# Seven block products for the up projections, and a normalization in place, in a two-layer trunk on one core

## The chip, the cores and the metric

The kernel runs on one core of one Trainium2 chip. The metric is the device time of one execution in microseconds. The profile pages and views come from one profiled execution; the names PE, PEld, DVE, ACT, POOL and SP stand for TensorE's matmuls, its weight loads, VectorE, ScalarE, GpSimd and SyncE. L12 is line 12 of the kernel.

## The reference

The input is x of shape (1, 512, 1024) in float32. Two layers follow; each has a mixer and a gated feed-forward network (FFN), both with an RMS norm ahead and a residual added behind. What the change touches is the FFN, the same in both layers, with 2816 hidden channels:

```python
def rms_norm(x, g):
    y = x * lax.rsqrt(jnp.mean(x * x, axis=-1, keepdims=True) + EPS)
    return y * g

def gated_conv_ffn(x, w_gate, w_up, conv_w, conv_b, w_down):
    g = jnp.einsum('bsd,df->bsf', x, w_gate)
    g = causal_dwconv3(g, conv_w) + conv_b          # three taps along the sequence
    up = jnp.einsum('bsd,df->bsf', x, w_up)
    return jnp.einsum('bsf,fd->bsd', jax.nn.silu(g) * up, w_down)

# in each layer, after its mixer:
hn = rms_norm(h, norm_ffn[layer])
h = h + gated_conv_ffn(hn, w_ffn_gate[layer], w_ffn_up[layer], conv_ffn[layer],
                       b_conv_ffn[layer], w_ffn_down[layer])
```

A final RMS norm gives the output.

## The kernel before, in words

The residual lies in SBUF as eight tiles `h[k]` of 128 channels by 512 positions. Every operand of a matmul is kept as two float32r tiles, a high half (a rounded copy, made by ScalarE) and a low half (the rest, a subtraction on VectorE). `mm3` (L125 to L128) makes one product of three matmuls: high by high, high by low, low by high. So each 128 x 128 x 512 product costs three matmuls of 512 columns.

`Norm.add` runs as each residual tile is finished: it writes `hg[k]`, the two halves of the tile times the norm's gain, and adds the tile's square to `ssq` (ScalarE squares, POOL adds). The factor rstd of each position is not in `hg`; it is multiplied in after the matmuls. `Norm.rstd` (L178) makes it as a tile of 128 x 512: two matmuls by a tile of ones, and then `inv_sqrt` on full tiles.

The FFN goes through 11 groups of two hidden tiles (f = 0, 2, ..., 20). `gate_up` fetches four weight tiles of 512 KB (the gate and up columns, in two halves of the channels) through a ring of four `raw` buffers on SP's queue, and `parts` (L118) splits each into a pair `whi`, `wlo`, from rings of five. Then it makes 96 matmuls into four PSUM banks: two gate tiles, two up tiles. Group 0 interleaves the four banks (tail 4), the others finish bank by bank. `done` takes each bank out: a gate bank is multiplied by rstd (L465), goes through the convolution (`conv3`, L231 to L233, VectorE), the silu (L469, ScalarE) and a product with rstd (L470, POOL); an up bank is multiplied with that (L474) and `split` gives the activation's two halves. After 12 groups' tiles, and again after the last 10 (`HALVES`), the down projection runs over the tiles so far: `project` in layer 0 (names d), `group8` over eight banks in layer 1 (names dn). In layer 1 the residual is also transposed back (`turn_residual`, 32 transposes named hT) between the groups f = 2 to 8.

The order of the instructions on each engine is fixed when the program is built: a scheduler takes them by the order written, and puts a later one first where an earlier one would have to wait. Buffers of one tag are handed out as they come free.

Of the kernel before, what the change touches and what calls it, by code (L numbers as in the profile page):

```python
# [15 lines left out]
P = 128  # L16
# [14 lines left out]
def tile_trunk(ctx: ExitStack, tc: tile.TileContext, x, norm_mix, norm_ffn, final_norm,  # L31
# [52 lines left out]

    def params(layer, rows_, queue=nc.sync):
        rows = sum(n for _, _, n in rows_)
        pk = cp.tile([P, P], F32, tag=f"pk{layer}", name=f"pk{layer}")
# [12 lines left out]

        return col
# [13 lines left out]
    def weights(src, a, b, name):  # L115
        return parts(*fetch(src, a, b, name))

    def parts(raw, a, b, name):  # L118
        hi = wp.tile([P, a, b], F32R, tag="whi", bufs=5, name=f"whi_{name}")
        lo = wp.tile([P, a, b], F32R, tag="wlo", bufs=5, name=f"wlo_{name}")  # L120
        nc.scalar.activation(hi, raw, AF.Copy)  # L121
        nc.vector.tensor_tensor(lo, raw, hi.bitcast(F32), ALU.subtract)  # L122
        return hi, lo
# [3 lines left out]
        nc.tensor.matmul(ps, lhs[0], rhs[1], start=False, stop=False)  # L127
        nc.tensor.matmul(ps, lhs[1], rhs[0], start=False, stop=stop)  # L128

    def group(name, outs, ks, lhs, rhs, tail, on_done, before=None):  # L130

        banks = {}
        head = len(ks) - tail
# [3 lines left out]
        for i, j in order:  # L137
            if i > at and before is not None:
                before(ks[i])
            at = max(at, i)  # L140
            if j not in banks:
                banks[j] = mm_bank(f"{name}_{j}")
            mm3(banks[j], lhs(ks[i], j), rhs(ks[i], j), i == 0, i == len(ks) - 1)
            if i == len(ks) - 1:
                on_done(j, banks[j])


    h = [cp.tile([P, S], F32, name=f"h{k}") for k in range(NK)]
# [6 lines left out]
    class Norm:  # L155


        def __init__(self, name, gain):
            self.name, self.gain, self.n = name, gain, 0
            self.ssq = tp.tile([P, S], F32, tag="ssq", bufs=1, name=f"ssq_{name}")  # L160

        def add(self, k):
# [6 lines left out]
        def square(self, k, order=lambda ins: ins):  # L169
            if self.n == 0:  # L170
                order(nc.scalar.activation(self.ssq, h[k], AF.Square))
            else:
                sq = tp.tile([P, S], F32, tag="sq", name=f"sq_{self.name}{k}")
                order(nc.scalar.activation(sq, h[k], AF.Square))
# [2 lines left out]

        def rstd(self):  # L178
            ps = aux_bank(f"ss_{self.name}")
            hi = tp.tile([P, S], F32R, tag=f"ms{S}", bufs=1, name=f"ssh_{self.name}")  # L180
            lo = tp.tile([P, S], F32R, tag=f"sd{S}", bufs=1, name=f"ssl_{self.name}")
# [6 lines left out]
            return r  # L188

        def rstd_cols(self):  # L190
# [3 lines left out]
                                 ones, start=True, stop=True)  # L194
            return inv_sqrt_cols(ps[:, :NT], NT, f"{self.name}c")

    def newton(ms, n, name, r):


        sd = tp.tile([P, max(n, LINE)], F32, tag=f"sd{max(n, LINE)}", bufs=1, name=f"sd_{name}")[:, :n]  # L200
# [4 lines left out]

    def inv_sqrt(r, ss, n, name):

        ms = tp.tile([P, max(n, LINE)], F32, tag=f"ms{max(n, LINE)}", bufs=1, name=f"ms_{name}")[:, :n]
# [98 lines left out]
    def mixer0():  # L307
        nonlocal prm0
        w = w_in_even[0]
        with tc.tile_pool(name="m0", bufs=1) as mp:  # L310
# [116 lines left out]

            in_group("ab", w, 0, True, b_done, 4)

            nxt = Norm("f0", lambda k: prm0("ffn", k))  # L430
# [6 lines left out]
    def gate_up(layer, prm, rstd, ap, acts, f, tail):  # L437

        cs = slice(f * P, (f + 2) * P)
        ch = {}  # L440
        for half in range(2):
            for key, w in (("g", w_ffn_gate), ("u", w_ffn_up)) if tail < NK else ():
                ch[key, half] = weights(w[layer][half * 512 : (half + 1) * 512, cs]
                                        .rearrange("(k p) c -> p k c", p=P), 4, 256,
                                        f"{key}{layer}_{f}_{half}")
        if tail == NK:
            for key, w in (("g", w_ffn_gate), ("u", w_ffn_up)):
                for half in range(2):
                    ch[key, half] = weights(w[layer][half * 512 : (half + 1) * 512, cs]
                                            .rearrange("(k p) c -> p k c", p=P), 4, 256,  # L450
                                            f"{key}{layer}_{f}_{half}")

        def lhs(k, j):
            hi, lo = ch["gu"[j // 2], k // 4]
            c = slice((j % 2) * P, (j % 2 + 1) * P)
            return hi[:, k % 4, c], lo[:, k % 4, c]

        gates = {}

        def done(j, ps):  # L460
            ft = f + j % 2
            r = rstd()
            if j < 2:
                t = padded_tile()
                nc.vector.tensor_tensor(t[:, 2:], ps, r, ALU.mult)  # L465
                c = ap.tile([P, S], F32, tag="c", bufs=2, name=f"c{layer}_{ft}")
                conv3(c, t, *(prm("cf", i * NF + ft) for i in range(3)))
                s = ap.tile([P, S], F32, tag="s", bufs=3, name=f"s{layer}_{ft}")
                nc.scalar.activation(s, c, AF.Silu, bias=prm("bf", ft))  # L469
                nc.gpsimd.tensor_tensor(s, s, r, ALU.mult)  # L470
                gates[j] = s
            else:
                s = gates[j - 2]
                nc.vector.tensor_tensor(s, ps, s, ALU.mult)  # L474
                acts[ft] = split(ap, s, f"a{layer}_{ft}", tag="a", bufs=12)

        group(f"gu{layer}_{f}", range(4), list(range(NK)), lhs, lambda k, j: hg_k(k), tail, done)

    def lazy_rstd(norm):
        got = []  # L480

        def get():
            if not got:
                got.append(norm.rstd())
            return got[0]

        return get

    def ffn0(norm):
        nonlocal prm1  # L490
        with tc.tile_pool(name="f0", bufs=1) as ap:
            rstd = lazy_rstd(norm)
            nxt = None
            for a, b in HALVES:
                acts = {}
                for f in range(a, b, 2):
                    gate_up(0, prm0, rstd, ap, acts, f, 4 if f == 0 else NK)
# [3 lines left out]
                project(f"d0_{a}", w_ffn_down[0], acts, list(range(a, b)), nxt)  # L501
            return nxt


    def mixer1(norm):
        w = w_in_odd[0]
        with tc.tile_pool(name="m1", bufs=1) as mp:
# [113 lines left out]
                    for j in ((4,), (5,), (6, 7))[k - 1]:  # L621
                        turned(j)

            nxt = Norm("f1", lambda k: prm1("ffn", k))
            project("oo", w_out_odd[0], mix, list(range(NK)), nxt, before=second_half)
            return nxt


    def ffn1(norm):
        with tc.tile_pool(name="f1", bufs=1) as ap:  # L630
            fin = ap.tile([P, D], F32, name="fin")
            nc.scalar.dma_start(fin, final_norm.rearrange("(o d) -> o d", o=1).to_broadcast([P, D]))
            rstd = lazy_rstd(norm)
# [3 lines left out]
            def turn_residual(t):  # L637
                for half in range(2):
                    ps = mm_bank(f"hT{t}_{half}")
                    for i in range(4):  # L640
                        nc.tensor.transpose(ps[:, i * P : (i + 1) * P],
                                            h[half * 4 + i][:, t * P : (t + 1) * P], ident)
                    nc.scalar.copy(y[t][:, half * 512 : (half + 1) * 512], ps)

            for a, b in HALVES:
                acts = {}
                for f in range(a, b, 2):
                    gate_up(1, prm1, rstd, ap, acts, f, 4 if f == 0 else NK)
                    if 2 <= f <= 8:
                        turn_residual((f - 2) // 2)  # L650
                last = b == NF
                if last:
                    root = small[:, 2:3]
                    nc.scalar.activation(root, eps, AF.Sqrt)
                ch = {}
# [88 lines left out]
```

## Time and profile before

| | |
|---|---|
| median of three runs | 1020.78 us (1020.74 to 1020.91) |
| the profiled execution | 1023.1 us, its span 1021.4 us |
| granted TensorE clock | 0.998 of full |
| hidden groups in layer 0 | from 147.98 and from 344.27 us |
| down projections in layer 0 | from 278.99 and from 453.11 us |
| hidden groups in layer 1 | from 651.04 and from 850.97 us |
| down projections in layer 1 | from 785.69 and from 959.77 us |
| DMA | 101.24 MB, mean 99 GB/s |

A group's row on the page gives the busy time, the mean length of one instruction and the idle time of the engine before it. Matmuls overlap: a record of 390 ns says how long one was in the array, not how often one can start.

### The profile page before, as it was taken

The page shows a single profiled execution, that of the slowest core. Times are in us where ns is not written, and L with a number is a line of the kernel's source. Part 1 is how long each engine was busy: PE and PEld are TensorE (multiplying, and loading weights), DVE is VectorE, ACT ScalarE, POOL GpSimd, SP SyncE. Part 2 cuts the span into 40 slices and gives each one's busy share as a digit, 9 for nine tenths or more (in the row PEclk, how much of TensorE's full clock was granted, in tenths as well). Part 3 has the DMA queues.
Part 4 walks back from the last instruction along what each step waited for, and adds up shares of the span by engine and source line. Part 5 has one row for each costly group of instructions (what it writes and reads, how often), then busy time and mean ns, then how long its engine had stood idle before and what let it go on. Part 6 is the DMA issues. An engine that isn't in the chain of part 4 may idle for free.

```text
span 1021.4 us, 11177 instructions
## 1 busy us (share of the span) xinstructions
PE 1009.4 (99%) x4485; PEld 832.4 (81%) x4485; DVE 559.0 (55%) x706; ACT 345.3 (34%) x449; POOL 126.7 (12%) x113
## 2 busy tenths in 40 slices
PE   9999999999999999999999999999999999999997
PEld 6788888888888888888878888888888888888885
DVE  5997567755623455654423645486554226565526
ACT  5423443323312223333345444433332212332313
POOL 3141121111100011111110001211111001111100
PEclk9999999999999999999999999999999999999999
DMA  7432233332333332332333123324233224233302
GB/s 232 154 103 83 83 103 98 92 115 89 95 111 84 96 109 83 103 104 78 106 126 103 62 91 96 103 83 124 83 103 103 84 81 124 83 104 103 100 3 83
DMA packets 74719, 101.24 MB, mean 99 GB/s; under 512 B 3268, under 2 KB 52652, under 8 KB 74668
## 3 DMA queue, kind: packets, MB, share of 16 engines
q1 hardware_dynamic: 73324, 98.96, 31.2%
q10 hardware_dynamic: 1344, 1.58, 0.5%
q8 instruction: 35, 0.57, 0.2%
q14 instruction: 16, 0.13, 0.0%
HBM read 98.42 MB, written 2.10 MB: 98 GB/s over the span
## 4 chain that ended last, share of the span: by engine, by line
PE 97%; DVE 1%; DMA 1%; issue 0%; POOL 0%; ACT 0%; DVEq 0%; POOLq 0%; ACTq 0%
PE gu L127 16%; PE gu L128 16%; PE gu L126 16%; PE dn L127 4%; PE d L126 4%; PE d L128 4%; PE dn L128 4%; PE d L127 4%; PE dn L126 4%; PE oo L128 1%; PE u L127 1%; PE u L126 1%; PE oo L127 1%; PE u L128 1%; PE oe L127 1%; PE oe L126 1%
## 5 line engine op out<-in xcount | busy, mean ns | idle before, releaser
L126 PE MATMUL gu<-hgh,whi_g 128*128 128x512 f32 x352 | 137.3, 390 | 0.0
L128 PE MATMUL gu<-hgh,wlo_g 128*128 128x512 f32 x352 | 137.0, 389 | 0.0
L128 PE MATMUL gu<-hgh,wlo_u 128*128 128x512 f32 x352 | 137.0, 389 | 0.0
L127 PE MATMUL gu<-hgl,whi_g 128*128 128x512 f32 x352 | 136.9, 389 | 0.0
L126 PE MATMUL gu<-hgh,whi_u 128*128 128x512 f32 x352 | 136.9, 389 | 0.0
L127 PE MATMUL gu<-hgl,whi_u 128*128 128x512 f32 x352 | 136.9, 389 | 0.0
L470 POOL TENSOR_TENSOR s<-s,rstd_f 128x512 f32<-128x512 f32 x44 | 66.5, 1512 | 529.8 <-ACT s L469 529.8
L121 ACT ACTIVATE whi_g<-raw_g 128x1024 fp32r<-128x1024 f32 x44 | 46.6, 1059 | 169.9 <-PE gu L127 107.8
L122 DVE TENSOR_TENSOR wlo_u<-raw_u,whi_u 128x1024 fp32r<-128x1024 f32 x52 | 63.8, 1229 | 59.5 <-ACT whi_u L121 59.1
L122 DVE TENSOR_TENSOR wlo_g<-raw_g,whi_g 128x1024 fp32r<-128x1024 f32 x44 | 54.4, 1236 | 47.3 <-ACT whi_g L121 46.9
L126 PEld LDWEIGHTS gu<-hgh,whi_u 128*128 128x128 f32 x352 | 66.1, 188 | 13.8
L127 PEld LDWEIGHTS gu<-hgl,whi_u 128*128 128x128 f32 x352 | 66.1, 188 | 13.7
L128 PEld LDWEIGHTS gu<-hgh,wlo_g 128*128 128x128 f32 x352 | 66.1, 188 | 13.7
L126 PEld LDWEIGHTS gu<-hgh,whi_g 128*128 128x128 f32 x352 | 66.1, 188 | 13.6
L128 PEld LDWEIGHTS gu<-hgh,wlo_u 128*128 128x128 f32 x352 | 66.1, 188 | 13.6
L127 PEld LDWEIGHTS gu<-hgl,whi_g 128*128 128x128 f32 x352 | 66.1, 188 | 13.6
L121 ACT ACTIVATE whi_u<-raw_u 128x1024 fp32r<-128x1024 f32 x52 | 55.0, 1059 | 58.6 <-PE gu L127 20.7
L126 PE MATMUL d<-a_hi,whi_d 128*128 128x512 f32 x176 | 68.6, 390 | 0.0
L128 PE MATMUL d<-a_hi,wlo_d 128*128 128x512 f32 x176 | 68.5, 389 | 0.0
L127 PE MATMUL d<-a_lo,whi_d 128*128 128x512 f32 x176 | 68.5, 389 | 0.0
L126 PE MATMUL dn<-whi_dn,a_hi 128*128 128x512 f32 x176 | 68.5, 389 | 0.0
L127 PE MATMUL dn<-wlo_dn,a_hi 128*128 128x512 f32 x176 | 68.5, 389 | 0.0
(236 smaller groups left out, 1772.5 us busy)
## 6 DMA issues: line engine op xcount, KB each, us to landing
raw_g<-in_w_ffn_gate_dram SPq DMA_DIRECT2D x44, 512.0 KB
raw_u<-in_w_ffn_up_dram SPq DMA_DIRECT2D x44, 512.0 KB, 3.9
raw_d<-in_w_ffn_down_dram SPq DMA_DIRECT2D x22, 512.0 KB, 3.5
raw_dn<-in_w_ffn_down_dram SPq DMA_DIRECT2D x22, 512.0 KB, 3.3
raw_oe<-in_w_out_even_dram SPq DMA_DIRECT2D x8, 512.0 KB, 3.3
raw_v<-in_w_in_odd_dram SPq DMA_DIRECT2D x8, 512.0 KB, 3.6
raw_u<-in_w_in_odd_dram SPq DMA_DIRECT2D x8, 512.0 KB, 3.5
raw_oo<-in_w_out_odd_dram SPq DMA_DIRECT2D x8, 512.0 KB, 3.3
```

Of the source, the lines that this page charges most:

```text
L121: nc.scalar.activation(hi, raw, AF.Copy)
L122: nc.vector.tensor_tensor(lo, raw, hi.bitcast(F32), ALU.subtract)
L126: nc.tensor.matmul(ps, lhs[0], rhs[0], start=start, stop=False)
L127: nc.tensor.matmul(ps, lhs[0], rhs[1], start=False, stop=False)
L128: nc.tensor.matmul(ps, lhs[1], rhs[0], start=False, stop=stop)
L470: nc.gpsimd.tensor_tensor(s, s, r, ALU.mult)
```

## The change

- From the third group on (f = 4 and up, nine groups in each layer) the up half is computed by a block scheme of seven products (`seven`). The up weights and the normalized tiles are cut in 2 x 2 blocks: the weights in two halves of the channels by two hidden tiles, the tiles in the same halves of the channels by two halves of the positions (256). Seven products of sums of blocks give the four blocks of the result. The sums of weight blocks (`s23`, `s14`) are made by VectorE in each group, the sums of the tiles (`t23`, `t41`) once per layer. The products 1, 6, 7 and 4 are added up in one PSUM bank, which is copied out in between (`keep`), 5 and 3 in another.
- The tiles must be normalized for that. `normalize(kp)` makes `hg[kp]` and `hg[kp + 4]` anew with rstd in them, in place, and the sums. It is written three times before and once after the evacuation of group 0 (`rest()`). Group 0 still works with rstd behind the matmuls, group 2 with normalized tiles and its gates ahead of its ups.
- `rstd` comes from 8 matmuls of one column (`rstd_tokens`), the root on 128 x 4, and four transposes that spread it (`rstd_spread`), at positions 2 and 4 of group 0. The last square is kept apart instead of added by POOL.
- Low halves of the tile sums and of one up weight half come from a DMA on POOL's queue that adds into its destination. The convolution's first step moves from VectorE to ScalarE. POOL's product with rstd remains in group 0 alone.
- The down projection runs in four parts (`PARTS`) instead of two. In layer 1 all residual transposes move into group 0. Some buffers share places: `t23` of layer 1 takes those of `h`; `final_norm` is loaded late.

```diff
-    HALVES = ((0, 12), (12, 22))
+    PARTS = ((0, 6), (6, 12), (12, 18), (18, 22))
+    HALF = S // 2
+    NP = NK // 2
+    PAIRS = [k for i in range(NP) for k in (i, i + NP)]
...
+    def summed(raw, a, b, name):
+        hi = wp.tile([P, a, b], F32R, tag="whi", bufs=5, name=f"whi_{name}")
+        lo = wp.tile([P, a, b], F32R, tag="wlo", bufs=5, name=f"wlo_{name}")
+        nc.scalar.activation(lo, raw, AF.Copy, scale=-1.0)
+        nc.gpsimd.dma_start(lo, raw, accum_op=ALU.add)
+        nc.scalar.activation(hi, raw, AF.Copy)
+        return hi, lo
...
+        def rstd_tokens(self):
+            ps = aux_bank(f"sst_{self.name}")
+            for t in range(NT):
+                ts_ = slice(t * P, (t + 1) * P)
+                nc.tensor.matmul(ps[:, t : t + 1], self.ssq[:, ts_], ones, start=True, stop=False)
+                nc.tensor.matmul(ps[:, t : t + 1], self.last[:, ts_], ones, start=False, stop=True)
+            self.cols = inv_sqrt_cols(ps[:, :NT], NT, f"{self.name}t")
...
+        def normalize(self, kp):
+            n, r = f"{self.layer}_{kp}", self.r
+            x = self.ap.tile([P, 2, S], F32, tag="sum", bufs=3, name=f"x{n}")
+            for i, k in enumerate((kp, kp + NP)):
+                nc.vector.scalar_tensor_tensor(x[:, i, :], h[k], self.prm("ffn", k), r,
+                                               op0=ALU.mult, op1=ALU.mult)
...
+            halves(hg[kp], x[:, 0, :])
+            halves(hg[kp + NP], x[:, 1, :])
...
+            nc.vector.tensor_tensor(t[:, 1, :], b22, b12, ALU.subtract)
+            nc.vector.tensor_tensor(t[:, 0, :], t[:, 1, :], b11, ALU.add)
+            nc.vector.tensor_tensor(t[:, 3, :], b12, b11, ALU.subtract)
+            nc.vector.tensor_tensor(t[:, 2, :], b21, t[:, 0, :], ALU.subtract)
...
+            for (hi, lo), src in ((self.t23[kp], t[:, :2, :]), (self.t41[kp], t[:, 2:, :])):
+                nc.scalar.activation(lo, src, AF.Copy, scale=-1.0)
+                nc.gpsimd.dma_start(lo, src, accum_op=ALU.add)
+                nc.scalar.activation(hi, src, AF.Copy)
...
+        def seven(self, f):
...
+            gate = [parts(*raws["g", 0])]
...
+            nc.vector.tensor_tensor(s14[:, 0], r0[:, :, P:], r1[:, :, P:], ALU.add)
+            nc.vector.tensor_tensor(s23[:, 0], s14[:, 0], r0[:, :, :P], ALU.subtract)
+            nc.vector.tensor_tensor(s23[:, 1], r0[:, :, :P], r0[:, :, P:], ALU.subtract)
...
+            gate.append(parts(*raws["g", 1]))
+            nc.vector.tensor_tensor(s14[:, 1], r1[:, :, :P], s23[:, 0], ALU.subtract)
...
+            hi, lo = summed(*raws["u", 1])
...
+            def multiply(product):
...
+                ps = banks[at][:, :HALF]
+                hi, lo = stat[product]
+                for kp in range(NP):
+                    b_hi, b_lo = self.moving(product, kp)
+                    a_hi, a_lo = hi[:, kp, :], lo[:, kp, :]
+                    for l, r, end in ((a_hi, b_hi, False), (a_hi, b_lo, False),
+                                      (a_lo, b_hi, kp == NP - 1)):
+                        nc.tensor.matmul(ps, l, r, start=at not in opened, stop=end,
+                                         skip_group_check=True)
+                        opened.add(at)
+                return ps
...
+            keep(0, multiply(1))
+            gates(0)                     # pairs 0, 4, 1, 5 of the channels
+            keep(1, multiply(6))
+            gates(1)                     # pairs 2, 6, 3, 7
...
+            keep(2, multiply(7))
...
+            ps = multiply(5)
+            p2 = multiply(2)
+            add(2, ps)
+            add(0, p2)
+            ps = multiply(4)
...
+            self.act(f + 1, s[1])
+            add(1, multiply(3))
...
+            self.act(f, s[0])
+
+        def hidden(self, f, before=lambda i: None):
+            if f == 0:
+                def first(i):
+                    before(i)
+                    if i == 2:
+                        self.norm.rstd_tokens()
+                    elif i == 4:
+                        self.r = self.norm.rstd_spread()
+
+                rest = self.direct(0, False, (range(4),), first)
+                for kp in range(NP - 1):
+                    self.normalize(kp)
+                rest()
+                self.normalize(NP - 1)
+            elif f == 2:
+                self.direct(2, True, ((0, 1), (2, 3)))()
+            else:
+                self.seven(f)
```

`direct(f, normed, sets)` is the former scheme with the channel tiles in the order of `PAIRS` (0, 4, 1, 5, 2, 6, 3, 7); `sets` says which banks are made together.

More of the change, by code (lines that the diff above doesn't have):

```diff
@@ L86, in params @@
         rows = sum(n for _, _, n in rows_)
-        pk = cp.tile([P, P], F32, tag=f"pk{layer}", name=f"pk{layer}")
+        pk = cp.tile([P, P], F32, tag="pk", bufs=1, name=f"pk{layer}")
         at, views = 0, {}
@@ L128, in mm3, with group @@
         nc.tensor.matmul(ps, lhs[1], rhs[0], start=False, stop=stop)
-    def group(name, outs, ks, lhs, rhs, tail, on_done, before=None):
+    def group(name, outs, ks, lhs, rhs, tail, on_done, before=None, at_end=None):
         banks = {}
@@ L143, in group @@
             mm3(banks[j], lhs(ks[i], j), rhs(ks[i], j), i == 0, i == len(ks) - 1)
-            if i == len(ks) - 1:
+            if i == len(ks) - 1 and at_end is None:
                 on_done(j, banks[j])
-    h = [cp.tile([P, S], F32, name=f"h{k}") for k in range(NK)]
+        if at_end is not None:
+            at_end()
+            for j in outs:
+                on_done(j, banks[j])
+    h = [cp.tile([P, S], F32, tag=f"h{k}", name=f"h{k}") for k in range(NK)]
     hg = [(cp.tile([P, S], F32R, name=f"hgh{k}"), cp.tile([P, S], F32R, name=f"hgl{k}"))
@@ L171, in square @@
                 order(nc.scalar.activation(self.ssq, h[k], AF.Square))
+            elif self.n == NK - 1 and self.apart:
+                self.last = tp.tile([P, S], F32, tag="last", bufs=1, name=f"last_{self.name}")
+                order(nc.scalar.activation(self.last, h[k], AF.Square))
             else:
@@ L188, in rstd, with rstd_spread @@
             return r
+        def rstd_tokens(self):
[5 more added lines that the diff above has]
+            self.cols = inv_sqrt_cols(ps[:, :NT], NT, f"{self.name}t")
+        def rstd_spread(self):
+            ps = aux_bank(f"ssr_{self.name}")
+            for t in range(NT):
+                nc.tensor.transpose(ps[:, t * P : (t + 1) * P],
+                                    self.cols[:, t : t + 1].to_broadcast([P, P]), ident)
+            r = tp.tile([P, S], F32, tag="rstd", name=f"rstd_{self.name}")
+            nc.scalar.copy(r, ps)
+            return r
         def rstd_cols(self):
@@ L206, in inv_sqrt @@
     def inv_sqrt(r, ss, n, name):
-        ms = tp.tile([P, max(n, LINE)], F32, tag=f"ms{max(n, LINE)}", bufs=1, name=f"ms_{name}")[:, :n]
+        ms = work("ms", n, name)
         nc.vector.tensor_scalar(ms, ss, 1.0 / D, EPS, op0=ALU.mult, op1=ALU.add)
@@ L428, in mixer0 @@
             in_group("ab", w, 0, True, b_done, 4)
-            nxt = Norm("f0", lambda k: prm0("ffn", k))
+            nxt = Norm("f0", lambda k: prm0("ffn", k), apart=True)
             project("oe", w_out_even[0], mix, [4, 5, 6, 7, 0, 1, 2, 3], nxt)
             return nxt
-    HALVES = ((0, 12), (12, 22))
-    def gate_up(layer, prm, rstd, ap, acts, f, tail):
-        cs = slice(f * P, (f + 2) * P)
[L440 to L463, printed above, removed]
-                t = padded_tile()
[L465 to L471, printed above, removed]
-            else:
[L473 to L487, printed above, removed]
+    PARTS = ((0, 6), (6, 12), (12, 18), (18, 22))
+    HALF = S // 2
+    NP = NK // 2
+    PAIRS = [k for i in range(NP) for k in (i, i + NP)]
+    def ffn_weights(layer, f, order):
+        cs = slice(f * P, (f + 2) * P)
+        return {(key, half): fetch(
+            (w_ffn_gate if key == "g" else w_ffn_up)[layer][half * 512 : (half + 1) * 512, cs]
+            .rearrange("(k p) c -> p k c", p=P), 4, 256, f"{key}{layer}_{f}_{half}")
+            for key, half in order}
@@ L491, in ffn0, with sums @@
         with tc.tile_pool(name="f0", bufs=1) as ap:
-            rstd = lazy_rstd(norm)
+            def sums(kp):
+                return [ap.tile([P, 2, HALF], F32R, name=f"t23{i}_{kp}") for i in "hl"]
+            ffn = Ffn(0, prm0, norm, ap, sums)
             nxt = None
-            for a, b in HALVES:
-                acts = {}
+            for a, b in PARTS:
                 for f in range(a, b, 2):
-                    gate_up(0, prm0, rstd, ap, acts, f, 4 if f == 0 else NK)
+                    ffn.hidden(f)
                 if b == NF:
@@ L500, in ffn0 @@
                     nxt = Norm("m1", lambda k: prm1("mix", k))
-                project(f"d0_{a}", w_ffn_down[0], acts, list(range(a, b)), nxt)
+                project(f"d0_{a}", w_ffn_down[0], ffn.acts, list(range(a, b)), nxt)
             return nxt
@@ L630, in ffn1, with sums, turn_residual, before @@
         with tc.tile_pool(name="f1", bufs=1) as ap:
-            fin = ap.tile([P, D], F32, name="fin")
-            nc.scalar.dma_start(fin, final_norm.rearrange("(o d) -> o d", o=1).to_broadcast([P, D]))
-            rstd = lazy_rstd(norm)
+            def sums(kp):
+                return [cp.tile([P, 2, HALF], F32R, tag=f"h{k}", name=f"t23_{k}")
+                        for k in (kp, kp + NP)]
+            ffn = Ffn(1, prm1, norm, ap, sums)
+            acts = ffn.acts
             y = [ap.tile([P, D], F32, name=f"y{t}") for t in range(NT)]
             ssf = ap.tile([P, NT, PAD], F32, name="ssf")[:, :, :2]
[L637 to L646, printed above, removed]
+            def turn_residual(t, half):
+                ps = mm_bank(f"hT{t}_{half}")
+                for i in range(4):
+                    nc.tensor.transpose(ps[:, i * P : (i + 1) * P],
+                                        h[half * 4 + i][:, t * P : (t + 1) * P], ident)
+                nc.scalar.copy(y[t][:, half * 512 : (half + 1) * 512], ps)
+            def before(k):
+                if k < 4:
+                    turn_residual(k, 0)
+                elif k < 8:
+                    turn_residual(k - 4, 1)
+            for a, b in PARTS:
                 for f in range(a, b, 2):
-                    gate_up(1, prm1, rstd, ap, acts, f, 4 if f == 0 else NK)
-                    if 2 <= f <= 8:
-                        turn_residual((f - 2) // 2)
+                    ffn.hidden(f, before=before)
                 last = b == NF
                 if last:
+                    fin = wp.tile([P, D], F32, tag="raw", bufs=4, name="fin")
+                    nc.scalar.dma_start(
+                        fin, final_norm.rearrange("(o d) -> o d", o=1).to_broadcast([P, D]))
                     root = small[:, 2:3]
```

141 lines of the change are left out of this document (135 added, 6 removed).

## The prediction

> **What bounds the kernel now.** I read the page first, then what TensorE waits for, then its timeline, then VectorE's groups, then the stretches by time. The page:
>
> ```profile
> PE 1009.4 (99%) x4485; PEld 832.4 (81%) x4485; DVE 559.0 (55%) x706; ACT 345.3 (34%) x449; POOL 126.7 (12%) x113
> ...
> PE 97%; DVE 1%; DMA 1%; issue 0%; POOL 0%; ACT 0%; DVEq 0%; POOLq 0%; ACTq 0%
> ```
>
> The second line is the chain that ended last: 97% TensorE. All its waits on other engines are in the start-up (clock, z) and at the head of mixer 1 (wst):
>
> ```profile
> PE wst L520 <- POOL ws L513: 1.5, 1, 1.5
> PE clock L56 <- DVE idle L53: 1.3, 1, 1.3
> PE z L126 <- ACT hgh L342: 1.1, 2, 0.8
> PE z L127 <- DVE hgl L344: 0.8, 1, 0.8
> ```
>
> Inside both FFNs TensorE never stops. So time is won only by TensorE occupying less time, and any wait that appears is lost in full. TensorE's price per matmul is the distance between starts, not the 390 ns of a record:
>
> ```profile
> 300.07 0.39 PE L126 MATMUL d<-a_hi,whi_d 128*128 128x512 f32 x1
> 300.30 0.39 PE L127 MATMUL d<-a_lo,whi_d 128*128 128x512 f32 x1
> ...
> 300.98 0.39 PE L127 MATMUL d<-a_lo,whi_d 128*128 128x512 f32 x1
> ```
>
> Four starts in 0.91 us: 0.2267 us for 512 columns. Short matmuls, from the chain in order of time:
>
> ```profile
> 528.18 0.79 PE ssc_m L193 x8
> ...
> 763.21 0.88 PE hT L641 x8
> ```
>
> With 128 columns (hT) one costs 0.109 us, with 1 column (ssc) 0.099 to 0.112: a floor that doesn't depend on the columns, so it belongs to the weight load that every matmul carries. And VectorE in the first two hidden groups of layer 0:
>
> ```profile
> 148.00:170.00 22.00, 22.00 (x99) 18.23 (x98) 14.79 (x13) 6.91 (x9) 2.55 (x2) 1.00 0.35 100
> 170.00:192.00 22.00, 22.00 (x99) 18.23 (x98) 19.57 (x27) 9.90 (x13) 6.89 (x4) 1.00 0.31 92
> ```
>
> The columns after the length are PE, PEld, DVE, ACT and POOL busy. VectorE already works 34.4 of these 44 us, and the change adds work just there.
>
> **Block products.** In 9 of 11 groups of each layer (18 in all) the up half, 48 matmuls of 512 columns (48 x 0.2267 = 10.88 us), becomes seven products of 4 x 3 = 84 matmuls of 256 columns. The gate half stays. No matmul of 256 columns is in the trace. Bounds: not under the floor, 0.109; not over the straight line between 0.109 at 128 and 0.2267 at 512 columns, which gives 0.148, if the price is a flat floor and then a slope. If all of 0.2267 shrinks with the columns it is 0.113. I take 0.120, from the start-up, where the same 512 columns go at one in 0.43 us:
>
> ```profile
> 2.08 0.15 PEld L56 LDWEIGHTS <-idle 128*128 128x128 bf16 x1 [0.28 <-issue]
> 2.51 0.15 PEld L56 LDWEIGHTS <-idle 128*128 128x128 bf16 x1 [0.28 <-issue]
> ```
>
> Half of that is 0.2135; the 0.013 by which 0.2267 exceeds it I take as fixed, so 0.107 + 0.013 = 0.120. Then 84 x 0.120 = 10.08 us, 0.80 a group, 14.4 us in 18 groups. The ends: 0.113 saves 24.5 us, 0.148 costs 28 us; break-even is at 10.88 / 84 = 0.1295.
>
> The Trainium skill, "TensorE: Matmul & The Clock Gate", section "Back-to-back issue gap", gives warm matmuls N columns at 2.4 GHz and a fixed 2.5 ns, 262 cycles for 256 columns. Its figure for 512 would be 0.216 us where the trace has 0.2267, so the measurement decides; by the page's 0.109 the saving would be an estimated 31 us.
>
> **rstd.** Per layer two 512-column matmuls go (0.45 us). In come 8 matmuls of one column in plain float32, which the ssc rows show as two each (8 records for 4), so 16 x 0.112 = 1.79 us, and 4 transposes, 0.44 us. Net 1.8 us, 3.6 us in all, all on TensorE. The small chain between them (five VectorE steps of 0.16 us, a root of 0.2 us, table loads of 1.28 us) lies under the 24 matmuls between pair positions 2 and 4 (5.4 us). VectorE loses the 3.35 us reciprocal and five 0.69 us steps.
>
> **The first two groups.** Count from the first matmul of group 0. Its 96 matmuls and the rstd work last 24.0 us; r is there at 13.7: 48 matmuls up to pair position 4 (10.9), the column matmuls (1.8), the transposes (0.4) and a copy (0.57). Each `normalize` costs VectorE two steps of 0.75 (as the c groups), two of 0.69, four of half width at an estimated 0.43 (between 0.16 for 4 columns and 0.69 for 512): 4.6 us; ScalarE six of 0.63, and POOL two accumulating DMAs. Three run before `rest()`, one after. Group 2 reads the tiles in the order of the pairs and wants the last at 24.0 + 8.2 = 32.2. VectorE must by then do 3 x 4.6 + 2.9 (the halves of the fourth) and one low half of the gate weights, 1.23: 17.9 us in 18.5. It just fits if nothing else comes first. But `rest()` stands ahead of the fourth: two evacuations (0.69), four convolution steps (0.75), two products and two low halves (0.7 each), 7.2 us. All of it first: 6.6 us of stall a layer. Its last 2.8 us wait for ScalarE's silu (0.72) and POOL's product (1.5), so others slip in: 3.8. Nothing in front: 0. I take 3 us, 6 in both layers. In layer 1 the 32 residual transposes (0.109 each, 3.5 us, no more than before) move into this group: VectorE gets that time as cover, but r comes some 2 us later, and the sums reuse h's tiles, so wait for those transposes.
>
> **The steady groups.** A group lasts 10.88 + 10.08 = 20.96 us. VectorE's 13.2 us a group become 15.7 (four low halves of 1.23, five half-tiles of 0.69, four convolution steps of 0.76, the rest evacuation); ScalarE's 6.9 become 13.2. Both fit. Six weight pairs pass through five slots, and both gate halves are now held until the gates end. The next group's second gate half gets the slot of product 4, 1.44 us before the group's end, and is wanted 2.8 us after it: 4.2 us for a copy of 1.06 and a low half of 1.23, beside 3.4 us of evacuation on VectorE. If all of that goes first: 1.5 us, at five joints a layer, 15 us. If not, 0, which I take: in the trace such a low half (193.02) starts between the product at 192.22 and its own low half at 194.16. The u half summed by DMA has its slot after product 1 and is wanted at 16.6 us: 14 us of cover; plain loads of the same 512 KB land in 3.3 to 3.9 us, at worst 9.8 in the start-up.
>
> **Nothing on the path.** Four parts instead of two add 16 evacuations of 0.69 us per layer, in projections where VectorE waits 2.03 us before each; without that cover the 32 would cost 22 us. POOL's 40 products of 1.5 us in the later groups go, which frees its queue for the DMAs. SP's loads change order, not number; final_norm's load only moves. The last part's four tiles leave no head, but the other banks' 5.4 us lie ahead of the late tile's chain of some 3 us.
>
> **The sum.** -14.4 + 3.6 + 6 = -4.8 us. The profiled execution took 1023.1 (span 1021.4); it would take 1018.3, and the median of 1020.8 becomes 1016.0. A measurement of this kernel tells about 0.2%, 2 us, from no change.
>
> **Rivals.** First, *the fast case*: the price is 0.113 and the first groups hold: -24.5 + 3.6 = -20.9, 999.9; with 3 us of stall a layer 1006. For it: 1 and 128 columns cost the same, so loads overlap matmuls fully. Against: 0.2267 is more than twice 0.109. The skill's page above would put it there too. Chance 0.15.
>
> Second, the *starved gates*, on the slow side: the gate weights' low half in group 2 is written after `normalize(3)`. If VectorE's queue keeps the written order, it comes after 24.0 + 3.4 + 7.2 + 4.6 + 1.2 = 40.4, while TensorE runs dry at 25.4: 15 us a layer, 30 instead of 6: about 1040. It decides from 5.4 us a layer, where the net saving of 10.8 us is gone. For it: VectorE is never free there. Against: every DMA sum holds a tile of the three `sum` buffers and so opens gaps, and the slot of the first gate half is free 4 us before group 0 ends. Part of it (7 to 10 us a layer: 1024 to 1030) is as likely as all of it. Chance 0.22.
>
> Third, *short matmuls that don't pay*: from 0.127 us the rstd cost is no longer earned back; at 0.148, with 6 us of stalls, 1020.8 + 28 + 9.6 = 1058. Chance 0.09.
>
> Fourth, the *late sum*: the accumulating DMA takes over 14 us, and product 2 waits for it; each us beyond costs 18 us, 3 us late means 1070. Against: the plain loads above. For it: POOL and VectorE do hinder each other here (a VectorE step of 0.75 took 1.77 us at 151.06, beside POOL's sum). "SBUF — State Buffer" of the Trainium skill warns that a DMA issued from GpSimd is starved while VectorE runs a two-port step; by it the sum would be late, but the kernel's one such step per tile, the convolution's first, moves to ScalarE. No run here shows it. Chance 0.04.
>
> Even: stalls of about 10 us eat the saving. Chance 0.08. The forecast itself, 1006 to 1018: 0.42.
>
> **Numbers.** Faster by over 0.2%: 0.42 + 0.15 = 0.57; within: 0.08; slower: 0.22 + 0.09 + 0.04 = 0.35. Likeliest 1016; its own range 1006 to 1018. From 1002 to 1036 leaves out the best end of the fast case, full starvation in both layers, and the costly matmuls.
>
> **What would show it.** Starts of the `u` matmuls 0.120 us apart; a steady group 21.0 us long; TensorE's waits listing VectorE's hgl and wlo_g in group 2 with some 6 us; no wait of TensorE on a DMA. A distance over 0.127, or waits of over 11 us in all, make the forecast wrong.

## The result and the profile after

The changed kernel took 1030.24 us (median of four runs, 1028.55 to 1031.83) against 1020.85 us for the kernel before beside it: a ratio of 1.0085, with a 95% interval of 1.006 to 1.011. It is slower by about 9 us, where 1016 was forecast. The profiled execution took 1031.83 us with a span of 1029.8 us, 8.4 us more than before.

The page's line of the engines, its line of clocks in 40 slices, and its chain that ended last:

```profile
PE 1004.6 (98%) x5169; PEld 856.7 (83%) x5169; DVE 609.5 (59%) x878; ACT 471.6 (46%) x689; POOL 93.8 (9%) x105
...
PEclk9999999899999999999999999999999999999998
...
PE 92%; DVE 4%; DMA 1%; ACT 1%; issue 1%; POOL 0%; SPq 0%; DVEq 0%; ACTq 0%; POOLq 0%
```

The chain has 5 points less of TensorE than before, and 4% VectorE. What TensorE waited for (total, times, longest):

```profile
PE gu L137 <- DVE wlo_g L131: 7.4, 1, 7.4
PE gu L135 <- ACT hgh L564: 3.7, 1, 3.7
PE gu L136 <- DVE hgl L565: 1.8, 1, 1.8
PE clock L56 <- DVE idle L53: 1.3, 1, 1.3
...
PE gu L135 <- DVE rows L544: 0.6, 1, 0.6
```

Before, no wait of TensorE lay in an FFN. Now four do, 13.5 us in all, and all in the first two groups (name gu): the first and the last in layer 0, the waits on hgh and hgl in layer 1. The stretches that the prediction read (PE, PEld, DVE, ACT, POOL busy, then the granted clock):

```profile
148.00:170.00 22.00, 22.00 (x109) 18.47 (x108) 12.15 (x26) 8.57 (x16) 3.08 (x3) 1.00 0.19 55
170.00:192.00 22.00, 14.02 (x53) 10.63 (x52) 19.01 (x32) 16.41 (x27) 8.76 (x8) 0.77 0.64 114
```

TensorE loses 8 us in the second stretch, and its clock is at 0.77 there. VectorE is busy for 12.15 us in the first stretch, where it was 14.79 before: it idles early and is full when it is needed. Its timeline shows both ends:

```profile
162.28 1.41 DVE L560 SCALAR_TENSOR_TENSOR x<-h,prm,rstd_f 128x512 f32<-128x512 f32 x2 [5.46 <-ACT rstd_f L222]
...
172.92 0.43 DVE L574 TENSOR_TENSOR t<-x 128x256 f32<-128x256 f32 x1 [1.23 <-DMA t<-t]
...
178.66 2.73 DVE L506 SCALAR_TENSOR_TENSOR c<-rows,prm,c 128x512 f32<-128x512 f32 x4
181.31 1.28 DVE L565 TENSOR_TENSOR hgl<-x,hgh 128x512 fp32r<-128x512 f32 x2
182.52 0.41 DVE L573 TENSOR_TENSOR t<-t,x 128x256 f32<-128x256 f32 x1
182.85 1.22 DVE L131 TENSOR_TENSOR wlo_g<-raw_g,whi_g 128x1024 fp32r<-128x1024 f32 x1
```

VectorE waits 5.46 us for rstd, then works through four normalizations, with two `rows` steps and four convolution steps of `rest()` among them, and waits 1.23 us for an accumulating DMA to give a `sum` buffer back. Only then comes the low half of group 2's gate weights. TensorE at the same place:

```profile
184.12 1.22 PE L137 MATMUL gu<-hgh,wlo_g 128*128 128x512 f32 x2 [7.42 <-DVE wlo_g L131]
185.15 0.63 PE L135 MATMUL gu<-hgh,whi_g 128*128 128x512 f32 x1
185.57 0.63 PE L136 MATMUL gu<-hgl,whi_g 128*128 128x512 f32 x1
186.00 0.63 PE L137 MATMUL gu<-hgh,wlo_g 128*128 128x512 f32 x1
...
188.12 0.39 PE L136 MATMUL gu<-hgl,whi_g 128*128 128x512 f32 x1
188.35 0.39 PE L137 MATMUL gu<-hgh,wlo_g 128*128 128x512 f32 x1
```

It had run dry at 176.70. After the gap the starts lie 0.427 us apart instead of 0.227, for eight matmuls: 1.6 us more. In layer 1 the place is the same and the cause another:

```profile
688.52 0.43 DVE L572 TENSOR_TENSOR t<-x 128x256 f32<-128x256 f32 x1 [3.89 <-DMA t<-t]
```

VectorE had the gate weights' low half done at 682 there, and TensorE never waited for it. But then VectorE stood 3.89 us for a buffer that an accumulating DMA held, in the midst of the third normalization, and the fourth came late (hgh 3.7, hgl 1.8 us of TensorE's waits).

The whole bill, from the distances between TensorE's starts: each matmul is given its usual distance (0.2267 us for 512 columns, 0.120 for 256, 0.109 and 0.112 for the short ones). What exceeds it by more than 0.1 us, and the half-clock matmuls, count as stall.

| us | before | after |
|---|---|---|
| FFN of layer 0: work, stall | 359.65, 0 | 354.21, 10.4 |
| FFN of layer 1: work, stall | 362.81, 0 | 357.37, 7.7 |
| small excesses in both FFNs | 0.1 | 1.8 |
| stall in mixer 1 | 1.7 | 0 |
| start and end | 14.4 | 15.6 |

Work -10.9, stalls +18.0 (before rounding), excesses +1.7, mixer 1 -1.7, start and end +1.2: +8.3 of the span's 8.4 us. The stall in mixer 1, a wait on POOL's `ws`, comes and goes between executions: it is 1.5 us in one of the kernels below that don't touch it, and 0.4 us or less in the others.

### The profile page after: what moved, and what is told of

The parts are those of the page before. It is cut to its first block, busy times and chain, and to the rows that moved or that the text cites. A ratio compares the mean times of both kernels' runs of the same rounds, so it can differ in the third digit from the quotient of the medians.

```text
span 1029.8 us, 12982 instructions
## 1 busy us (share of the span) xinstructions
PE 1004.6 (98%) x5169; PEld 856.7 (83%) x5169; DVE 609.5 (59%) x878; ACT 471.6 (46%) x689; POOL 93.8 (9%) x105
## 4 chain that ended last, share of the span: by engine, by line
PE 92%; DVE 4%; DMA 1%; ACT 1%; issue 1%; POOL 0%; SPq 0%; DVEq 0%; ACTq 0%; POOLq 0%
PE ua L649 10%; PE g L136 6%; PE g L135 6%; PE g L137 6%; PE ue L649 5%; PE d L136 4%; PE d L135 4%; PE d L137 4%; PE dn L135 4%; PE dn L136 4%; PE dn L137 4%; PE ub L649 3%; PE gu L137 2%; PE gu L136 2%; PE gu L135 2%; PE v L135 1%
## 5 line engine op out<-in xcount | busy, mean ns | idle before, releaser
L135 PE MATMUL g<-hgh,whi_g 128*128 128x512 f32 x288 | 112.5, 391 | 0.0
L136 PE MATMUL g<-hgl,whi_g 128*128 128x512 f32 x288 | 112.5, 391 | 0.0
L137 PE MATMUL g<-hgh,wlo_g 128*128 128x512 f32 x288 | 112.1, 389 | 0.0
L137 PE MATMUL dn<-whi_dn,a_lo 128*128 128x512 f32 x176 | 68.3, 389 | 0.0
L506 DVE SCALAR_TENSOR_TENSOR c<-rows,prm,c 128x512 f32<-128x512 f32 x88 | 63.5, 746 | 1.2 <-ACT c L504 0.6
L137 PEld LDWEIGHTS g<-hgh,wlo_g 128*128 128x128 f32 x288 | 54.1, 188 | 11.9 <-DVE wlo_g L131 0.5
L135 PEld LDWEIGHTS g<-hgh,whi_g 128*128 128x128 f32 x288 | 54.2, 188 | 10.4
L136 PEld LDWEIGHTS g<-hgl,whi_g 128*128 128x128 f32 x288 | 54.2, 188 | 9.8
L131 DVE TENSOR_TENSOR wlo_d<-raw_d,whi_d 128x1024 fp32r<-128x1024 f32 x22 | 26.8, 1219 | 36.1 <-ACT whi_d L130 36.1
L605 ACT ACTIVATE whi_s<-s 128x1024 fp32r<-128x1024 f32 x36 | 38.1, 1057 | 16.6 <-PE d L136 14.2
```

Of the source, the lines that this page charges most:

```text
L135: nc.tensor.matmul(ps, lhs[0], rhs[0], start=start, stop=False)
L506: nc.vector.scalar_tensor_tensor(c, t[:, i : S + i], prm("cf", i * NF + ft), c, op0=ALU.mult, op1=ALU.add)
L605: nc.scalar.activation(hi, src, AF.Copy)
```

## The experiments

Theory at first: the stalls of the first groups are the order and the amount of work on VectorE between rstd and group 4 (V). Rivals: the accumulating DMAs and the buffers that they hold (D); the block products pay less than their price says; the normalization itself is the cost. Each ratio stands against the kernel before on the same chip, with its 95% interval.

**Gate weights of group 2 early.** They are prepared right behind group 0's matmuls, ahead of the normalizations:

```diff
                 rest = self.direct(0, False, (range(4),), first)
+                self.ch2 = self.prepare(2, ((0, 1), (2, 3)))
                 for kp in range(NP - 1):
                     self.normalize(kp)
...
-                self.direct(2, True, ((0, 1), (2, 3)))()
+                self.direct(2, True, ((0, 1), (2, 3)), ch=self.ch2)()
```

> The weights of group 2 are fetched and split right behind group 0's matmuls in the written order, ahead of normalize and rest; nothing else is changed. Theory A (the loss is VectorE's queue in the first two groups): TensorE's 7.4 us wait on wlo_g in layer 0 goes, and with it the 1.5 us of half clock behind it; layer 1, which waits on hgh and hgl, keeps its 5.5 us: 1030.2 becomes 1020 to 1023. Theory B (the loss is in the groups of block products, and the first two groups would lose as much in another place): within 2 us of 1030.

1022.46 us, ratio 1.001 (0.9997 to 1.0024). The 7.4 us wait is gone, and what is left, but for 0.9 us in group 4, are waits for the last tiles:

```profile
PE gu L136 <- DVE hgl L569: 4.2, 2, 2.1
PE gu L135 <- ACT hgh L568: 2.7, 1, 2.7
```

That is within what was expected. Layer 0's stall falls from 10.4 to 3.9 us, layer 1's only from 7.7 to 6.9. So the place of the gate weights explains layer 0's larger half, and hardly anything of layer 1.

**The tile sums' low halves by VectorE instead of the DMA,** on top of that:

```diff
-                nc.scalar.activation(lo, src, AF.Copy, scale=-1.0)
-                nc.gpsimd.dma_start(lo, src, accum_op=ALU.add)
                 nc.scalar.activation(hi, src, AF.Copy)
+                nc.vector.tensor_tensor(lo, src, hi.bitcast(F32), ALU.subtract)
```

> As e1_gates_early, and the low halves of the tile sums are subtracted by VectorE instead of added by a DMA on POOL's queue, so that the sum buffers come free sooner. VectorE gets 16 more steps of 0.69 us in all. Theory A, with the DMA's hold on the buffers as layer 1's cause: the 3.9 us in which VectorE waits for the DMA in layer 1 go, TensorE's waits on hgh and hgl shrink from 5.5 us to under 2: 1015 to 1019. If VectorE's work itself is the bound in layer 1: no better than e1_gates_early, 1020 to 1024.

1029.66 us, ratio 1.008 (1.0064 to 1.0096): a miss, above both ranges. Most of the waits leave group 2 and come back in group 4, for weight sums that VectorE makes too late. The waits, and VectorE in the stretches up to there:

```profile
PE ua L652 <- ACT whi_s L608: 8.2, 2, 5.3
```

```profile
170.00:192.00 22.00, 21.13 (x93) 16.97 (x92) 20.80 (x36) 12.19 (x17) 3.71 (x2) 1.00 0.23 72
192.00:206.00 14.00, 8.56 (x39) 6.83 (x38) 14.00 (x22) 10.81 (x17) 0.00 (x0) 0.78 0.23 76
```

VectorE is the third pair behind the length: 20.80 of 22 and 14.00 of 14 us. Taking the DMA away moves its work to the engine that has no time. Here the DMA earns its place.

**No block products.** `self.seven(f)` becomes `self.direct(f, True, ((0, 1), (2, 3)))()`.

> All groups from the third on use the direct matmuls on normalized tiles; the sums of the tiles are still made and not used. Theory A: each of 18 groups costs 0.80 us more (48 x 0.2267 instead of 84 x 0.120), the first two groups as in the changed kernel: 1030.2 + 14.4 = 1044.6, between 1042 and 1047. Theory B (the block products lose what they save by the work around them): 1028 to 1033.

1043.06 us, ratio 1.0213 (1.0198 to 1.0228), with the same 7.4 us wait in group 2. The block products are worth about 13 us of time (1043.06 - 1030.24). In the bill the work of an FFN rises by 7.21 us, 14.4 us for both, as forecast.

**No normalization in place.** The sums are made of the tiles times the gain alone, and rstd is multiplied in behind the matmuls in every group, as before the change; `rest()` stands behind all four sums:

```diff
-                nc.vector.scalar_tensor_tensor(x[:, i, :], h[k], self.prm("ffn", k), r,
-                                               op0=ALU.mult, op1=ALU.mult)
...
+                nc.scalar.activation(x[:, i, :], h[k], AF.Copy, scale=self.prm("ffn", k))
...
-                nc.scalar.copy(t[:, 2:], banks[j])
+                nc.vector.tensor_tensor(t[:, 2:], banks[j], self.r, ALU.mult)
...
                 s.append(self.silu(c[j], f + j))
+                nc.gpsimd.tensor_tensor(s[j], s[j], self.r, ALU.mult)
```

> Block products on tiles that are not normalized: the sums are made from h times the gain (ScalarE scales), nothing is written in place, rstd comes in behind the matmuls in all groups (VectorE takes the gate banks out, POOL multiplies the silu, as in the kernel before). Theory A: no wait of TensorE in the first two groups, so 1020.8 - 14.4 + 3.6 = 1010, between 1008 and 1014. Theory B: the groups of block products lose as before, over 1020.

1030.69 us, ratio 1.009 (1.0073 to 1.0106): a miss for A. B's "over 1020" came, but not its reason, a loss "as before": in the changed kernel no joint of the later groups (a joint is where one group ends and the next begins) waits. Here the first two groups no longer stall, but all ten joints between steady groups do, nine by 0.6 us and one by 1.7, and the third group of layer 1 by 3.7 us:

```profile
PE g L137 <- DVE wlo_g L131: 4.0, 10, 0.7
PE g L135 <- ACT whi_g L130: 3.7, 1, 3.7
```

POOL's product with rstd stands at the end of each group, and VectorE's queue behind it:

```profile
290.80 0.42 DVE L686 TENSOR_TENSOR s<-kept,s 128x256 f32<-128x256 f32 x1 [1.19 <-POOL s L680]
...
291.81 1.21 DVE L131 TENSOR_TENSOR wlo_g<-raw_g,whi_g 128x1024 fp32r<-128x1024 f32 x1
```

So normalizing in place is not the mistake: against this form, which leaves a factor to POOL and VectorE in every group, it keeps the steady joints free. What it lacks is time in the first two groups. The 3.7 us of layer 1 were not taken apart.

**rstd earlier.** By now V said that VectorE's idle time before rstd (5.46 us) is what lacks later; D, that layer 1 has a cause of its own. Both are tried, alone and together:

```diff
-                    if i == 2:
+                    if i == 1:
                         self.norm.rstd_tokens()
-                    elif i == 4:
+                    elif i == 2:
                         self.r = self.norm.rstd_spread()
```

> The changed kernel with rstd about 5.4 us earlier and nothing else. Theory V: the gate weights of group 2 still stand behind three normalizations in VectorE's queue, but all of that begins 5.4 us earlier: layer 0's gap of 7.7 us falls to about 2.3 us, with the half-clock matmuls 10.4 to 3 or 4; layer 1's 7.7 to 3 to 5: 1030.2 - 6.5 - 3.7 = 1020 us, 1017 to 1023. Theory D: 1024 to 1028.

The changed kernel with this alone: 1023.21 us, ratio 1.0001 (0.9992 to 1.001), by the ratios some 8 us better than the change, 0.2 us above V's range and below D's. Its profiled run was its fastest (1020.62); there layer 0 stalls 3.0 and layer 1 5.0 us.

> e1_gates_early with the rstd columns computed at the second pair of group 0 and spread at the third (they were at the third and the fifth): in e1_gates_early VectorE stood idle for 5.5 us (layer 0) and 6.4 us (layer 1) until rstd was there, and it is ready about 5.4 us earlier now. Theory V (what VectorE has to do between rstd and the first matmuls of group 4 is the limit): the gaps that e1_gates_early still had, 3.9 us in layer 0 and 6.9 us in layer 1 with the half-clock matmuls, shrink by about as much as rstd comes earlier: to 0 to 1 us and to 1.5 to 3 us. 1022.5 - 3.4 - 4.6 = 1014.5 us, 1013 to 1017. Theory D (what holds VectorE up is the buffers that the accumulating DMAs keep, and in layer 1 the slots of h, which are free only when the residual's transposes have ended at the eighth pair): layer 0 gains 1 to 3 us, layer 1 nothing, since its first tile waits for h's slots as before: 1019 to 1021.5 us.

With the early gate weights: 1018.81 us, ratio 0.997 (0.996 to 0.998), above V's range and just below D's. V was right about layer 0, whose stall is 0. Layer 1's is 4.9 us: it gained 2.0, where D expected no gain and V some 4 to 5:

```profile
PE gu L135 <- ACT hgh L568: 2.8, 1, 2.8
...
PE gu L136 <- DVE hgl L569: 1.6, 1, 1.6
```

**The residual's transposes of layer 1 earlier.** Its first tile sums (`t23`) take the slots of `h`, which these transposes read until the eighth pair:

```diff
             if k < 4:
                 turn_residual(k, 0)
-            elif k < 8:
-                turn_residual(k - 4, 1)
+                turn_residual(k, 1)
```

> e1_gates_early with all 32 transposes of layer 1's residual at the first four pairs (they were spread over eight), so that h's slots, where layer 1 puts its first tile sums, are free some 11 us earlier, about when rstd is ready. Theory D: layer 1's gaps, 6.9 us in e1_gates_early, fall to 2 to 4 us, what layer 0 has: 1018 to 1020 us. Theory V: the accumulating DMAs start earlier, but VectorE's work before group 4 stays as it was; layer 1 loses only the time for which VectorE waited for DMA, 2.1 + 0.8 us: 1019 to 1021 us. Neither effect, or the denser transposes delay the group's matmuls: 1022 to 1024 us.

With the early gates, but rstd as in the change: 1021.63 us, ratio 0.9998 (0.9989 to 1.0007). Layer 1's stall falls from 6.9 to 4.5 us, layer 0's stays (4.2), and mixer 1 waits 1.7 us again. The time is above the ranges of both. Layer 1's gain of 2.4 us is less than either said (V 2.9, D 2.9 to 4.9), so this run alone doesn't decide between them.

> e8_early_gates_and_rstd with the residual's 32 transposes of layer 1 at the first four pairs; the evacuation of group 0 stays between the third and the fourth normalization. e8_early_gates_and_rstd stalls in layer 1 alone, 4.9 us. If the place that its first tile sums take (h's slots, which the transposes read until the eighth pair) is what is left, the stall falls to 0 to 1.5 us: 1013.5 to 1015.5 us. If it is the evacuation standing ahead of the last normalization, 1017 to 1019 us.

With early gates, early rstd and early transposes: 1012.98 us (1012.36 to 1013.66), ratio 0.9919 (0.9902 to 0.9937), 0.5 us below the range for the slots. TensorE's waits, all that the view lists:

```profile
PE z L135 <- ACT hgh L382: 1.6, 2, 0.8
PE clock L56 <- DVE idle L53: 1.3, 1, 1.3
PE z L136 <- DVE hgl L384: 0.8, 1, 0.8
PE wst L754 <- POOL ws L747: 0.4, 1, 0.4
```

No wait in either FFN, and about 8 us less than the kernel before: a version that beats both. How it works is in POOL's queue of layer 1, which issues the accumulating DMAs. First with early gates and rstd alone, then with the transposes early:

```profile
663.79 0.86 POOL L585 DMA_DIRECT2D t<-t  x1 [1.69 <-ACT t L584]
672.01 0.86 POOL L585 DMA_DIRECT2D t<-t  x1 [7.36 <-ACT t L584]
```

```profile
661.99 0.86 POOL L585 DMA_DIRECT2D t<-t  x1 [0.16 <-issue]
663.55 0.86 POOL L585 DMA_DIRECT2D t<-t  x1 [0.70 <-ACT t L584]
```

ScalarE's copies into h's slots had to wait for the transposes (in the first kernel the last one starts at 670.0), so the third DMA was issued at 672 instead of 663.5, and VectorE's buffer came back late: VectorE stood 2.95 us for it, up to 677.91.

**The order of `rest()`.** It goes behind all four normalizations:

```diff
-                for kp in range(NP - 1):
+                for kp in range(NP):
                     self.normalize(kp)
                 rest()
-                self.normalize(NP - 1)
```

> e8_early_gates_and_rstd with the evacuation of group 0 behind all four normalizations; the transposes of layer 1's residual stay spread over eight pairs. If h's slots are what is left in layer 1, its stall of 4.9 us stays at 3 to 5 us: 1017 to 1019 us. If the order is, it falls to 0 to 1.5: 1013.5 to 1015.5 us.

With early gates and rstd, transposes as in the change: 1015.49 us, ratio 0.9942 (0.9926 to 0.9957). The time is at the upper end for the order. Layer 1 stalls 2.2 us instead of 4.9, between the two readings: the order alone takes away 2.7 us there, the slots alone all of it.

> Gates of group 2 early, rstd early, the residual's transposes in the first four pairs, and the evacuation of group 0 behind all four normalizations. If VectorE's work and the buffers are together what stalls the first groups, both layers' stalls fall to 0 to 1.5 us: the sum without stalls is 1020.9 - 10.9 + 1 to 2 us of drag and end, 1011 to 1014 us. If the evacuation of group 0, now last, holds up group 4's weights in VectorE's queue, 1014 to 1018.

All four together: 1013.23 us (1012.28 to 1014.24), ratio 0.9909 (0.9894 to 0.9924), no stall in either FFN, as expected. With rstd and the transposes early, the order of `rest()` has nothing left to give.

**The old rstd in the best kernel.** `rstd()` as before the change, two 512-column matmuls and the chain on full tiles, at the third pair:

> e12_early_and_turns with rstd computed as before the change (the two 512-column matmuls, and the chain on 512 columns: 0.69 + 0.69 + 3.35 + 3 x 0.69 = 6.8 us of VectorE by the rows of the kernel before), called at the third pair of group 0. TensorE saves the 24 short matmuls: 1.8 us a layer, 3.6 us in all. Theory V: rstd is ready some 7 us later than in e12_early_and_turns, at about 162 us as in e1_gates_early, and VectorE has 6 us more to do before that; the stalls come back to at least the 4.2 and 4.5 us of e9_early_gates_and_turns, more if VectorE's extra work counts in full: 1013 - 3.6 + 9 to 15 = 1018 to 1024 us. If VectorE's lateness costs nothing here, 1009 to 1010 us.

1019.43 us, ratio 0.9974 (0.9963 to 0.9986), within what V said. The work of each FFN falls by 1.78 us, but the stalls are 5.3 and 6.3 us. VectorE before its first normalization:

```profile
154.26 0.69 DVE L249 TENSOR_SCALAR ms_f<-ss_f 128x512 f32<-128x512 f32 x1 [0.60 <-PE ss_f L201]
155.71 3.35 DVE L242 RECIPROCAL rstd_f<-sd_f 128x512 f32<-128x512 f32 x1 [0.76 <-ACT sd_f L241]
...
161.28 1.42 DVE L564 SCALAR_TENSOR_TENSOR x<-h,prm,rstd_f 128x512 f32<-128x512 f32 x2
```

The first tile is normalized at 161.28 instead of 155.66. rstd by columns costs TensorE 3.6 us and gives back some 11.6 us of stalls; as a time the old form is 6.4 us slower. An earlier place for the old form was not tried.

## Why the prediction was wrong

**The step that failed is "The first two groups", "I take 3 us, 6 in both layers".** It measured 10.4 + 7.7 us, 18.0 before rounding. The sum of -4.8 thus became +7.2, and the small rest (excesses, mixer 1, both ends) made it +8.4. Three things in the step went wrong:

- *One due time for all the work* (layer 0). It set 17.9 us of VectorE against 18.5 us up to the last tile, and counted the gate weights' low half among it. But TensorE wants that half 6.8 us before the last tile by the prediction's own numbers (25.4 and 32.2). It ran dry at 176.7, while the step came at 182.85, behind nearly all of the four normalizations. The amount of work was not short: two normalizations took 8.0 us where 9.2 were priced. The starved-gates rival had the right due time (dry at 25.4 after the start, in the trace 28.4) and the right order. It asked for all of `rest()` ahead, and only six of its ten steps were. Its part of 7 to 10 us a layer, 1024 to 1030, was close to what came (10.4, 7.7 and 1030.24), but for layer 1 by luck: the gates were not late there. Putting the gates first took 6.5 us out of layer 0 and 0.8 out of layer 1, so this cause is shown for layer 0.
- *Buffers as a help* (layer 1 above all). "Every DMA sum holds a tile of the three `sum` buffers and so opens gaps" was counted against the rival. In layer 1 that came true, and the gates' half went ahead of the last two sums. But the gaps are also VectorE's lost time: 1.23 us in layer 0 and 3.89 in layer 1. The prediction named the slots of `h` and gave them no price; with the transposes early, layer 1's remaining 4.9 us went to 0.
- *The clock.* The half clock after a gap had no price. It is 1.6 us for eight matmuls in each layer.

The idle 5.46 us before rstd was in the prediction as well (rstd at 13.7), without the conclusion that it is VectorE's time which can be had: early rstd alone was worth some 8 us.

**What was right.** The price of a 256-column matmul: the starts in a steady group are 0.120 us apart.

```profile
258.83 0.28 PE L649 MATMUL ua<-hgl,whi_a 128*128 128x256 f32 x1
258.95 0.28 PE L649 MATMUL ua<-hgh,wlo_a 128*128 128x256 f32 x1
259.07 0.28 PE L649 MATMUL ua<-hgh,whi_a 128*128 128x256 f32 x1
```

The Trainium skill, "TensorE: Matmul & The Clock Gate", section "Back-to-back issue gap", would have it at 0.109 us by its formula for an isolated warm matmul; the trace does not agree, and the fast case that rested on less than 0.120 falls, like the short matmuls that don't pay. The 0.80 us a group and 14.4 us in all are what the bill shows between block products and none. rstd's 1.8 us a layer is the 1.78 that came back with the old form. A steady group lasts 20.99 us (258.36 to 279.35), where 20.96 was forecast, and its joints cost nothing. The late sum did not happen:

```profile
wlo_u<-raw_u POOLq DMA_DIRECT2D x18, 512.0 KB, 4.6
```

4.6 us to land (the median) where 14 were free. The evacuations of two more projections a layer left no wait. And the sum without stalls, 10.8 us below before: the span of the kernel with early gates, rstd and transposes is 1010.7 us, 10.7 below 1021.4. That the two agree so well is partly luck. The profiled execution of the kernel before was 2.3 us above its median, and the medians on one chip are 8.3 us apart (1021.28 and 1012.98). In the two FFNs alone the profiles show 9.4 us, the 10.9 of work less 1.5 of small excesses, which the prediction had at nothing.

## What to carry to other kernels

Give each item of an off-path engine's queue its own due time: the sum of the work may fit while the item that is wanted first stands last. When a step makes an engine do much in a short time, first look for what holds back its start; here moving the start forward 5 us, at no cost in work, was worth as much as ordering the queue. And a buffer that is shared with an earlier reader, or held by a DMA, is part of the engine's time in such a stretch.

## What the runs showed of the hardware

- After a gap TensorE's starts at 512 columns went from 0.227 to 0.427 us for some microseconds. This followed gaps of 7.5 us (eight matmuls), but also of 2.2 us (seven, with early gates and transposes), while after 2.9 and 1.8 us (early gates and rstd) none was slow. So the length of a gap alone doesn't decide it, from 2 to 3 us: one of 2.96 us (rstd early alone, layer 1) was followed by five slow ones, one of 2.94 (early gates and rstd, layer 1) by none. What decides it was not tried. The Trainium skill, "TensorE: Matmul & The Clock Gate", section "Part 1: The HAM clock gate", speaks of a free-running window of about 3.4 us, and half rate after at least one idle window. The 7.5 us agree; the 2.2 us are shorter than the window and were followed by the half rate nevertheless.
- An accumulating DMA of 256 KB within SBUF landed in 3.2 to 8.6 us, while the 512 KB one of the steady groups took 4.6 in the median. Which of its neighbours slowed the long ones wasn't tried.
- A 128 x 256 step of VectorE is recorded with 0.42 us, but the next one starts 0.34 us later. The prediction took the records (0.69, 0.75, and for this step an estimated 0.43) as the price, which was too much: two normalizations together took 8.0 us (162.28 to 170.28), not 9.2. As with TensorE's matmuls, the price is the distance of the starts.
